# An MoE block on one core: four slots' expert rows go through DRAM and are fetched per token, in place of one-hot products

## The chip, the core and the metric

The kernel runs on one core of a Trainium2 chip. Times are device microseconds of one launch, from the first to the last instruction and what lies around them, as the runtime gives them. TensorE (PE) has two clock levels, 1.2 and 2.4 GHz; the profile gives the granted share of the higher one.

## What is computed

512 tokens of width 1024 pass a layer norm, a token mixer (convolution and pooling), a second layer norm that gives `h`, a mixture of 32 experts, a gated per-layer embedding and a last layer norm. The change is in the mixture:

```python
g_idx = top1(tok @ w_rg + b_rg)                      # one of 4 groups
top_v, top_i = top_k(e_logits_of_that_group, 2)      # two of its 8 experts
act = silu(tok @ w_gate[e]) * (tok @ w_up[e]) * combine[e]
moe = sum_e act @ w_down[e]                          # two experts per token
ple = (p @ w_ple) * sigmoid(h @ w_pg + b_pg)
out = layernorm(alpha * h + moe + ple)
```

An expert has 3 MB of float32 weights, all 32 have 96 MB, and each is read once.

## The kernel before, in words

Experts are ranked by how many tokens they have, and ranks are packed into 12 slots of 128 rows (`SLOTS`, from `ORDER_S`). A slot holds four experts of 32 rows ("q", and slot 0), two of 64 ("p"), or one of 96 and one of 32 ("h"). The slots run in the order 0, q, h, p, q, h, p, q, p, p, p, p, so slots 2 to 5 are h, p, q, h.

For each slot `s` the main loop does the following on PE. `gate_up` (L1043) multiplies the slot's gathered and transposed rows with the gate and up weights, in two halves of the contraction. `xtr` (L1032) transposes the next slot's rows. `act` makes the activation on ACT and DVE and, on DVE, a one-hot matrix `oh` of the tokens that the rows belong to (L1061). `atr` (L1066) transposes the activation. `down` (L1083) multiplies with the down weights; its result is copied out of PSUM by ACT as a rounded high part and by DVE as the low rest (L1091, L1093). One slot later `scatter` (L1105, L1107) takes the rows back to the 512 tokens: for each of 4 chunks of tokens and 2 halves of the width one product of `oh` with the high and one with the low part, 16 matmuls of 128x512 per slot, and DVE adds each PSUM result to `tok` (L1108). Chunks 0 and 1 stand between the halves of the next slot's `gate_up`, chunks 2 and 3 around its `atr`.

Weights come in pieces of 1 MB by SP's DMA queue (`pump`, L667; `W`, tile `w_x`), three for each expert, in the order of the slots. They are put into one of about 14 buffers, each given back (`done`) when PE has read it; `keep` holds some buffers back for other uses. A load waits for its buffer, and for the load eight issues earlier. Rows of the slot three ahead are gathered from DRAM (`h1d`) by an indirect DMA on POOL (`gather`, L1023), which skips rows that have no token.

The embedding gate's products (`q_pg`, L807, L815, L818) are filler: 160 "quanta", one product of 128x256 each, put between the other work. `fill(n)` places `n` of them. `fill_until(keys)` places as many as fit before a weight piece is expected, by the account `clk`: `clk["pe"]` adds up the assumed time of PE's work, `clk["dma"]` that of the loads. So the account, at build time, sets where the quanta stand; on the chip nothing is moved. 30 of them stand ahead of slot 0. At slot 9 `fill(999)` places all that are left, since later work needs the finished `tok`. From slot 9 on `tok` is also split into high and low parts for the last norm (`split_tok`), and slot 11 overlaps its own last steps with the norm and the stores.

## Time and profile before

| | us |
|---|---|
| median of 3 runs (lowest, highest) | 479.41 (478.61, 481.82) |
| the profiled execution | 477.51 |
| its span, first to last instruction | 475.7 |
| PE busy in the span | 444.1 |

The profile is of one execution. Engines are PE (matmul), PEld (its weight loads), DVE, ACT, POOL and SP; a "q" behind the name is the engine's sequencer, which issues DMAs. A matmul's modelled duration overlaps the next one's, so PE's work is best read from the starts in the timeline. The slots' part begins at 197 us and ends at about 463 us.

### The profile page before, as it was taken

The numbers are of one execution on the slowest core, as the hardware profiler recorded it, in microseconds if no ns is written. First come the engines' busy times: TensorE is split into PE (matmuls) and PEld (weight loads), VectorE is DVE, ScalarE is ACT, GpSimd is POOL, SyncE is SP. The second block draws the span as 40 slices with busy tenths as digits, with TensorE's granted clock in tenths as the row PEclk, the third lists the DMA queues.
The fourth block names the chain that finished last, engine by engine and source line by source line (L and its number), as shares of the span: only waits on it lengthen the run. The fifth ranks groups of instructions, "written<-read, shape, count | busy, mean of one in ns | idle before, by whom it ended". The sixth has DMA issues, their size and how long they took to land.

```text
span 475.7 us, 7009 instructions
## 1 busy us (share of the span) xinstructions
PE 444.1 (93%) x2647; PEld 297.7 (63%) x2647; DVE 253.4 (53%) x493; ACT 131.0 (28%) x240; POOL 141.8 (30%) x121
## 2 busy tenths in 40 slices
PE   7899979999999998898879999999999999999990
PEld 6798857788899997542425446644556458454430
DVE  4939599879664776322424422443433361354695
ACT  4562512341400585220202211211201121241260
POOL 2557499327403640320001000100001011432094
PEclk8999997999999998999989999999999999999995
DMA  8822204222876797499999999999999999486013
GB/s 265 340 91 89 90 1 167 99 100 96 332 285 253 250 352 282 161 372 421 416 425 419 420 418 421 420 421 418 418 422 420 421 417 417 182 252 234 1 44 148
DMA packets 23389, 133.20 MB, mean 280 GB/s; under 512 B 3329, under 2 KB 3589, under 8 KB 10040
## 3 DMA queue, kind: packets, MB, share of 16 engines
q1 hardware_dynamic: 20456, 124.64, 65.9%
q0 software_dynamic: 2608, 6.50, 3.6%
q10 hardware_dynamic: 288, 1.57, 0.8%
q8 instruction: 22, 0.36, 0.3%
q14 instruction: 15, 0.12, 0.1%
HBM read 130.41 MB, written 4.72 MB: 284 GB/s over the span
## 4 chain that ended last, share of the span: by engine, by line
PE 39%; DMA 14%; DVE 2%; issue 1%; ACT 1%; POOL 1%; POOLq 0%; SPq 0%; DVEq 0%; ACTq 0%
DMA w_x<-wx_in 14%; PE g_gu L1043 14%; PE q_pg L815 7%; PE u_y L1083 6%; PE u_sc L1105 4%; PE u_sc L1107 3%; PE q_pg L807 2%; PE t_xt L1032 2%; PE q_zr L1322 1%; PE t_at L1066 0%; DVE tok L1364 0%; POOL tok L1352 0%; DVE tok L1359 0%; ACT L1340 0%; POOLq L1545 0%
## 5 line engine op out<-in xcount | busy, mean ns | idle before, releaser
L1043 PE MATMUL g_gu<-w_x,xT 128*32 128x512 f32 (+1 forms) x544 | 84.0, 607 | 5.6 <-DMA w_x<-wx_in 5.4
L1108 DVE TENSOR_TENSOR tok<-tok,u_sc 128x512 f32<-128x512 f32 x88 | 55.3, 680 | 54.1 <-PE u_sc L1107 54.0
L360 PE MATMUL u_u<-hTh,ws 128*128 128x512 f32 (+1 forms) x320 | 67.6, 355 | 0.5 <-DVE ws L245 0.3
L360 PEld LDWEIGHTS u_u<-hTh,ws 128*128 128x128 f32 x320 | 53.9, 193 | 9.3 <-DVE ws L245 0.8
L1043 PEld LDWEIGHTS g_gu<-w_x,xT 128*32 128x32 f32 (+1 forms) x544 | 22.5, 119 | 56.8 <-issue 47.9
L815 PE MATMUL q_pg<-w_pg,h1T 128*128 128x256 f32 x240 | 58.1, 385 | 0.0
L815 PEld LDWEIGHTS q_pg<-w_pg,h1T 128*128 128x128 f32 x240 | 45.8, 193 | 9.1 <-issue 2.5
L1023 POOL DMA_INDIRECT xrow<-h1d,idxm x12 | 12.3, 1022 | 117.6 <-PE t_xt L1032 108.5
L1083 PE MATMUL u_y<-w_x,aT 128*32 128x512 f32 (+1 forms) x272 | 41.1, 596 | 0.0
L1105 PE MATMUL u_sc<-y,oh 128*128 128x512 f32 x88 | 40.4, 459 | 0.0
L826 POOL TENSOR_TENSOR tok<-tok,sgp 128x256 f32<-128x256 f32 x16 | 11.5, 724 | 85.4 <-DVE sgp L825 78.4
L184 PE MATMUL u_o<-ws,yTh 128*128 128x256 f32 x128 | 36.7, 287 | 0.3 <-ACT yTh L443 0.3
L186 PE MATMUL u_o<-ws,yTl 128*128 128x256 f32 x128 | 36.3, 284 | 0.6 <-DVE yTl L444 0.6
L360 PE MATMUL u_u<-hTl,ws 128*128 128x512 f32 (+1 forms) x160 | 35.3, 351 | 1.2 <-DVE hTl L345 1.2
L185 PE MATMUL u_o<-ws,yTh 128*128 128x256 f32 x128 | 36.2, 283 | 0.0
L1093 DVE TENSOR_TENSOR y<-u_y,y 128x512 fp32r<-128x512 f32 x22 | 15.2, 692 | 37.0 <-ACT y L1091 37.0
L1107 PE MATMUL u_sc<-y,oh 128*128 128x512 f32 x88 | 34.7, 394 | 0.0
L360 PEld LDWEIGHTS u_u<-hTl,ws 128*128 128x128 f32 x160 | 27.5, 192 | 5.7 <-DVE hTl L345 1.6
L1052 ACT ACTIVATE sa<-g_gu 128x256 f32<-128x256 f32 x12 | 4.6, 382 | 96.0 <-PE g_gu L1043 96.0
L245 DVE TENSOR_TENSOR ws<-raw,ws 128x1024 fp32r<-128x1024 f32 (+1 forms) x19 | 25.3, 1365 | 9.8 <-ACT ws L242 9.8
L1105 PEld LDWEIGHTS u_sc<-y,oh 128*128 128x128 f32 x88 | 16.6, 189 | 15.7 <-issue 8.2
L1055 DVE TENSOR_TENSOR sa<-g_gu,sa 128x256 f32<-128x256 f32 x12 | 5.1, 422 | 39.3 <-ACT sa L1052 39.3
(273 smaller groups left out, 682.9 us busy)
## 6 DMA issues: line engine op xcount, KB each, us to landing
w_x<-wx_in SPq DMA_DIRECT2D x89, 1024.0 KB, 20.4
raw<-win_in SPq DMA_DIRECT2D x6, 1024.0 KB, 6.2
w_half<-wx_in SPq DMA_DIRECT2D x12, 512.0 KB, 7.3
raw<-wout_in SPq DMA_DIRECT2D x4, 1024.0 KB, 4.7
w_pg<-wpg_in SPq DMA_DIRECT2D x4, 1024.0 KB, 20.2
raw<-win_in SPq DMA_DIRECT2D x4, 512.0 KB, 6.8
bc<-rows_in SPq DMA_DIRECT2D x4, 512.0 KB, 9.6
h1d<-tok POOLq DMA_DIRECT2D x3, 512.0 KB, 7.2
```

Source lines behind the costliest of these rows:

```text
L184: PE.matmul(o, lh, rh, start=start, stop=False)
L185: PE.matmul(o, lh, rl, start=False, stop=False)
L186: PE.matmul(o, ll, rh, start=False, stop=stop)
L245: eng.tensor_sub(wsp[n][1][j][:, ks], raws[n][:, j, ks], wsp[n][0][j][:, ks].bitcast(F32))
L360: PE.matmul(o[:, ns], (l if p == 2 else h)[j][:, kn], (hTl if p == 1 else hTh)[k][:, ns], start=i == 1, stop=i == 3 * KD)
L815: PE.matmul(g, h1T[:, k, cs], W["pg", j, 0][0][:, k * 256:(k + 1) * 256], start=(k == 0), stop=False)
L1043: PE.matmul(g[q:q + m, :], xTs[s][:, k, q:q + m], W["x", r, kh][0][:, (k % 4) * 512:(k % 4 + 1) * 512], start=(k == 0), stop=(k == KD - 1) ...
L1083: PE.matmul(yp[h][q:q + m, :], aTs[s][:, c, q:q + m], W["x", r, 2][0][:, c * D + h * 512:c * D + (h + 1) * 512], start=(c == 0), stop=(c = ...
L1093: V.tensor_sub(yl[:, hs], yp[h], yh[:, hs].bitcast(F32))
L1105: PE.matmul(o, ohs[s][:, c * P:(c + 1) * P], yh[:, w], start=True, stop=yl is None)
L1107: PE.matmul(o, ohs[s][:, c * P:(c + 1) * P], yl[:, w], start=False, stop=True)
L1108: V.tensor_add(tok[:, c, w], tok[:, c, w], o)
```

## The change

Slots 2 to 5 (`DS`) are no longer scattered by one-hot products. `down` copies their rows (ACT the first half, DVE the second) into one half of the tile `yrows`, and ACT's queue writes them to the DRAM tensor `yd`, 512 KB for each slot. Slot indices of each token's two experts are put into `yix`, shifted so that those outside slots 2 to 5 lie out of bounds. For each chunk of 128 tokens, `blank` zeroes a tile of two rows per token on ACT (in a weight buffer), `fetch` reads the rows of `yd` by two indirect DMAs on POOL, which skip indices out of bounds, and `collect` adds the two to `tok` on DVE (128x1024 each). Chunks 0 and 1 are blanked and fetched in slot 6 and added in slot 7; chunks 2 and 3 are blanked and fetched behind slot 7 and added in slot 8. `keep` holds back two buffers from slot 5 on for that. The other slots keep the one-hot products.

The account's numbers are changed (3.7 in place of 3.45, and so on; the start of the slots' account is -1.5 ahead of slot 0 where it was 8.0 behind it), so that quanta are placed elsewhere.

```diff
@@ -70,6 +70,8 @@
 NS = len(SLOTS)
 NOV = 8
 NL = NS + 1
+DS0, DS1 = 2, 6
+DS = range(DS0, DS1)
 MORE = NS * P - 32
 
 
@@ -177,6 +179,7 @@
     eps_t = const.tile([P, 1], F32, name="eps_t")
     sgn = const.tile([P, 1], F32, name="sgn")
     h1d = dram.tile([1 + T, D], F32, name="h1d")
+    yd = dram.tile([len(DS) * P, D], F32, name="yd")
     SLOT = {}
 
 
@@ -968,12 +971,14 @@
     V.scalar_tensor_tensor(g5, g5, BIG, pos3[:, :, 0:NST], OP.mult, OP.add)
     V.scalar_tensor_tensor(g4, g5, float(MORE), g4, OP.add, OP.min)
     gq = sm("gq", 2 * NC, E)
+    glist = {}
 
     def lists(gp, iotas, ns, nm, oq):
 
         V.tensor_tensor(gq.rearrange("p (i c) e -> p i c e", i=2), A12,
                         gp.unsqueeze(1).broadcast_to([P, 2, NC, E]), OP.mult)
         gi, si = sm("gi", 2 * NC, 1, dt=I32), sm("si", 2 * NC, 1, dt=I32)
+        glist[nm] = gi
         with nc.allow_low_precision(reason="whole numbers"):
             V.tensor_reduce(gi, gq, AX.X, OP.add)
         V.tensor_scalar(si, gi, 7, None, OP.arith_shift_right)
@@ -1043,7 +1048,7 @@
                 PE.matmul(g[q:q + m, :], xTs[s][:, k, q:q + m],
                           W["x", r, kh][0][:, (k % 4) * 512:(k % 4 + 1) * 512],
                           start=(k == 0), stop=(k == KD - 1), tile_position=(0, q))
-        clk["pe"] += 3.45
+        clk["pe"] += 3.7
         done(*[("x", r, kh) for r in dict.fromkeys(r for _, _, r in lanes)])
 
     def act(s, wsl, tkf, i, oh=None, sa=None):
@@ -1057,6 +1062,8 @@
         acts[s] = sa
         if s == NS - 1:
             return
+        if s in DS:
+            return
         ohs[s] = tmp("cv", 2, [P, T], f"oh{s}", F32R) if oh is None else oh
         V.tensor_scalar(ohs[s], C["iota"], tkf[:, i:i + 1], None, OP.is_equal)
 
@@ -1071,7 +1078,11 @@
         if s == NS - 1:
             y2 = ys[s] = tmp("x2", 1, [P, 2, 512], f"y{s}")
         else:
-            if y2 is None:
+            if s in DS:
+                if s == DS0:
+                    ys["d"] = tmp(ytags[0], 1, [P, 2, D], "yrows")
+                y2 = ys["d"][:, s % 2, :]
+            elif y2 is None:
                 y2 = tmp(ytags[0], 1, [P, 2, D], f"y{s}", F32R)
                 ys[s] = yh, yl = y2[:, 0, :], y2[:, 1, :]
             else:
@@ -1088,11 +1099,37 @@
             if s == NS - 1:
                 A.copy(y2[:, h, :], yp[h])
                 continue
+            if s in DS:
+                (A.copy if h == 0 else V.tensor_copy)(y2[:, hs], yp[h])
+                continue
             A.copy(yh[:, hs], yp[h])
             if yl is not None:
                 V.tensor_sub(yl[:, hs], yp[h], yh[:, hs].bitcast(F32))
-        clk["pe"] += 3.6
+        if s in DS:
+            A.dma_start(yd[(s - DS0) * P:(s - DS0 + 1) * P, :], y2)
+            clk["dma"] += 1.25
+        clk["pe"] += 3.75
         done(*[("x", r, 2) for r in dict.fromkeys(r for _, _, r in lanes)])
+
+    ygs = {}
+
+    def blank(c):
+
+        tag = free.pop(0) if c < 2 else ygs[c - 2][1]
+        yg = tmp(tag, 1, [P, 2, D], f"yg{c}")
+        ygs[c] = (yg, tag)
+        A.mul(yg.rearrange("p i (a n) -> p (i a) n", a=2), C["iota"].unsqueeze(1).broadcast_to([P, 4, 512]), 0.0)
+
+    def fetch(c):
+        clk["dma"] += 0.9
+        for i in range(2):
+            G.indirect_dma_start(out=ygs[c][0][:, i, :], out_offset=None, in_=yd,
+                                 in_offset=bass.IndirectOffsetOnAxis(ap=yix[:, i * NC + c, :], axis=0),
+                                 bounds_check=len(DS) * P - 1, oob_is_err=False)
+
+    def collect(c):
+        for i in range(2):
+            V.tensor_add(tok[:, c, :], tok[:, c, :], ygs[c][0][:, i, :])
 
     def scatter(s, cs=range(NC), mid=None, hs=(0, 1)):
         yh, yl = ys[s]
@@ -1106,7 +1143,7 @@
                 if yl is not None:
                     PE.matmul(o, ohs[s][:, c * P:(c + 1) * P], yl[:, w], start=False, stop=True)
                 V.tensor_add(tok[:, c, w], tok[:, c, w], o)
-            clk["pe"] += 0.88
+            clk["pe"] += 1.15
 
     xrow = [tmp(f"x{i}", 1, [P, D], f"xrow{i}") for i in range(2)]
     eid = s32("eid", 1, dt=I32)
@@ -1170,6 +1207,10 @@
     for gated, _ in hold[1:]:
         gated()
     wsl = slot_weights(oq, osl, NL, "m", tmp("cv", 2, [P, T], "oqb").bitcast(BF16))
+
+    yix, yin = sm("yix", 2 * NC, 1, dt=I32, tag="L"), sm("yin", 2 * NC, 1, tag="mg")
+    V.tensor_scalar(yin, glist["m"], float(DS0 * P), BIG, OP.is_lt, OP.mult)
+    V.scalar_tensor_tensor(yix, glist["m"], -float(DS0 * P), yin, OP.add, OP.add)
 
     def reload(spare):
         for k in spare:
@@ -1445,16 +1486,20 @@
     gather(2, idx, 2)
     pump()
     fill(FILLB)
+    clk["pe"] = -1.5
     gate_up(0, SLOTS[0], 0)
     fill(FILLC)
     gate_up(0, SLOTS[0], 1)
-    clk["pe"] = 8.0
     for s in range(NS):
         lanes = SLOTS[s]
         rs = list(dict.fromkeys(r for _, _, r in lanes))
         end = s == NS - 1
         if s in KEEP:
             keep[0] = KEEP[s]
+        if s == DS1:
+            keep[0] = 0
+            for c in range(2):
+                blank(c)
         if s == NS - 3:
             fill(999)
             last_load()
@@ -1477,7 +1522,8 @@
             gate_up(s, lanes, 0)
             if s == NS - 4:
                 t = token_row(t)
-            scatter(s - 1, (0, 1))
+            if s - 1 not in DS:
+                scatter(s - 1, (0, 1))
             if s == NS - 4:
                 selectors(t)
                 keep[0] = 2
@@ -1495,14 +1541,28 @@
         xtr(s + 1)
         if s + 3 < NS:
             gather(s + 3, idx, s + 3)
-        if s:
+        if s == DS1:
+            for c in range(2):
+                fetch(c)
+        if not s:
+            fill(FILL0)
+        elif s - 1 in DS:
+            fill(FILLD)
+        else:
             scatter(s - 1, (2,))
-        else:
-            fill(FILL0)
         atr(s)
-        clk["pe"] += 1.2
-        if s:
+        clk["pe"] += 1.35
+        if s and s - 1 in DS:
+            fill(FILLD)
+        elif s:
             scatter(s - 1, (3,), lambda: fill(MIDF))
+        if s == DS1 + 1:
+            for c in range(2):
+                collect(c)
+        if s == DS1 + 2:
+            for c in range(2, 4):
+                collect(c)
+                free.append(ygs[c][1])
         if s == NS - 3:
             split_tok(2, G)
             split_tok(3, G)
@@ -1511,9 +1571,14 @@
         if s == NS - 2:
             take(s - 1, ys[s - 1])
         down(s, lanes)
-
-
-KEEP = {NS - 4: 3}
+        if s == DS1 + 1:
+            for c in range(2, 4):
+                blank(c)
+                fetch(c)
+
+
+KEEP = {DS1 - 1: 2, NS - 4: 1}
+FILLD = 2
 MIDF = 4
 LNP = 512
 WLAG = 2.0
```

The three pieces below show how this comes out. On PE in slot 3 (`t_at` is the transposed activation, `u_sc` a scatter product, `q_pg` filler, `u_y` the down product), the rows from `atr` to the first down product were, before:

```order
L1066 MATMUL t_at_3068<-par,sa_3038 128x128 x2
L1105 MATMUL u_sc_3073<-y_2970,oh_2920 128x512
L1107 MATMUL u_sc_3073<-y_2970,oh_2920 128x512
L815 MATMUL q_pg_2967<-w_pg_0_1755,h1T 128x256 x4
L1105 MATMUL u_sc_3081<-y_2970,oh_2920 128x512
L1107 MATMUL u_sc_3081<-y_2970,oh_2920 128x512
L815 MATMUL q_pg_2967<-w_pg_0_1755,h1T 128x256 x2
L1083 MATMUL u_y_3088<-w_x_2_2817,aT_3071 64x512
```

On the same engine and place they are now:

```order
L1037 MATMUL t_xt_3053<-par,xrow_1888 128x128 x4
L818 MATMUL q_pg_2981<-w_pg_0_1756,h1T 128x256 x2
L1073 MATMUL t_at_3064<-par,sa_3042 128x128 x2
L818 MATMUL q_pg_2981<-w_pg_0_1756,h1T 128x256 x4
L821 MATMUL q_pg_2981<-bpg,bm 128x256
L1094 MATMUL u_y_3077<-w_x_2_2825,aT_3067 64x512
```

The scatter products are gone, and filler alone covers the wait for the activation. On PE between slot 8's down product and slot 9's first `gate_up` (`g_gu`) there stood, before, among others:

```order
L1083 MATMUL u_y_3966<-w_x_2_3712,aT_3944 64x512
L807 MATMUL q_pg_3982<-wple_3190,pT_1077 128x256
L807 MATMUL q_pg_3982<-wple_3190,pT_1078 128x256
L815 MATMUL q_pg_3982<-w_pg_0_2821,h1T 128x256 x8
L818 MATMUL q_pg_3982<-bpg,bm 128x256
L807 MATMUL q_pg_3997<-wple_3190,pT_1077 128x256
L807 MATMUL q_pg_3997<-wple_3190,pT_1078 128x256
L815 MATMUL q_pg_3997<-w_pg_0_2821,h1T 128x256 x8
L818 MATMUL q_pg_3997<-bpg,bm 128x256
```

Now, on PE at that place, the two follow each other:

```order
L1144 MATMUL u_sc_3902<-y_3738,oh_3673 128x512
L1094 MATMUL u_y_3911<-w_x_2_3643,aT_3896 64x512
L1094 MATMUL u_y_3911<-w_x_2_3645,aT_3896 64x512
L1094 MATMUL u_y_3911<-w_x_2_3643,aT_3896 64x512
L1094 MATMUL u_y_3911<-w_x_2_3645,aT_3896 64x512
L1094 MATMUL u_y_3912<-w_x_2_3643,aT_3896 64x512
L1094 MATMUL u_y_3912<-w_x_2_3645,aT_3896 64x512
L1094 MATMUL u_y_3912<-w_x_2_3643,aT_3896 64x512
L1094 MATMUL u_y_3912<-w_x_2_3645,aT_3896 64x512
L1048 MATMUL g_gu_3940<-w_x_0_3647,xT_3869 64x512
```

All 30 quanta that stood there have moved ahead of slot 8. On DVE in slot 8 (`tok<-tok,u_sc` adds a scatter product, `y` is the low part of the slot's own down product) there was, before:

```order
L1056 SCALAR_TENSOR_TENSOR sa_3911<-g_gu_3853,sa_3911 128x256
L1061 TENSOR_SCALAR oh_3915<-par,tkfm 128x512
L1108 TENSOR_TENSOR tok<-tok,u_sc_3933 128x512
L1108 TENSOR_TENSOR tok<-tok,u_sc_3937 128x512
L1108 TENSOR_TENSOR tok<-tok,u_sc_3946 128x512
L1108 TENSOR_TENSOR tok<-tok,u_sc_3954 128x512
L825 TENSOR_TENSOR sgp_3797<-q_pg_3796,sgp_3797 128x256
L1093 TENSOR_TENSOR y_3964<-u_y_3965,y_3964 128x512
L1093 TENSOR_TENSOR y_3964<-u_y_3966,y_3964 128x512
```

On DVE in slot 8 there is now, with the additions of fetched rows (`yg`):

```order
L1061 SCALAR_TENSOR_TENSOR sa_3863<-g_gu_3796,sa_3863 128x256
L1068 TENSOR_SCALAR oh_3867<-par,tkfm 128x512
L1145 TENSOR_TENSOR tok<-tok,u_sc_3885 128x512
L1145 TENSOR_TENSOR tok<-tok,u_sc_3889 128x512
L1145 TENSOR_TENSOR tok<-tok,u_sc_3898 128x512
L1145 TENSOR_TENSOR tok<-tok,u_sc_3902 128x512
L1132 TENSOR_TENSOR tok<-tok,yg_3778 128x1024 x2
L1132 TENSOR_TENSOR tok<-tok,yg_3786 128x1024 x2
L1107 TENSOR_TENSOR y_3910<-u_y_3911,y_3910 128x512
L1107 TENSOR_TENSOR y_3910<-u_y_3912,y_3910 128x512
```

The four additions of fetched rows stand ahead of the low part that slot 8's scatter needs in slot 9.

## Rows read from the trace of the kernel before

**Rows 1.** The page: busy time of the engines; granted clock and DMA in slices.

```profile
PE 444.1 (93%) x2647; PEld 297.7 (63%) x2647; DVE 253.4 (53%) x493; ACT 131.0 (28%) x240; POOL 141.8 (30%) x121
...
PEclk8999997999999998999989999999999999999995
DMA  8822204222876797499999999999999999486013
```

**Rows 2.** Busy time by stretch: us, the engines, granted clock, DMA share, GB/s.

```profile
247.00:374.00 127.00, 127.00 (x767) 68.87 (x765) 48.87 (x86) 21.07 (x44) 11.85 (x14) 1.00 1.01 420
374.00:407.00 33.00, 32.68 (x153) 21.15 (x151) 12.84 (x34) 4.04 (x9) 3.18 (x4) 1.00 0.99 412
407.00:445.00 38.00, 37.98 (x172) 17.63 (x172) 17.17 (x27) 10.06 (x17) 12.60 (x12) 1.00 0.54 185
...
239.00:247.00 8.00, 6.53 (x35) 1.80 (x36) 0.00 (x0) 0.00 (x0) 0.00 (x0) 0.79 1.02 424
```

**Rows 3.** Waits of SP's queue: us in total, times, longest.

```profile
SPq L667 <- DMA w_x<-wx_in: 105.6, 59, 2.7
```

**Rows 4.** Timeline of PE at slots 1 and 2: start, us, idle before.

```profile
222.65 3.62 PE L1043 MATMUL g_gu<-w_x,xT 128*32 128x512 f32 x26 [1.44 <-DMA w_x<-wx_in]
...
239.05 1.06 PE L1043 MATMUL g_gu<-w_x,xT 128*32 128x512 f32 x6 [2.50 <-DMA w_x<-wx_in]
241.53 4.92 PE L1043 MATMUL g_gu<-w_x,xT 128*32 128x512 f32 x26 [1.42 <-DMA w_x<-wx_in]
...
248.55 3.64 PE L1043 MATMUL g_gu<-w_x,xT 128*32 128x512 f32 x32
```

**Rows 5.** Timeline of PE in slot 6: eight scatter products, then gate_up.

```profile
330.84 0.50 PE L1105 MATMUL u_sc<-y,oh 128*128 128x512 f32 x1
...
333.01 3.65 PE L1043 MATMUL g_gu<-w_x,xT 128*64 128x512 f32 x16
```

**Rows 6.** Timeline of PE: first of slot 9's 30 quanta, then its gate_up.

```profile
393.57 1.13 PE L807 MATMUL q_pg<-wple,pT 128*128 128x256 f32 x4
...
407.07 3.65 PE L1043 MATMUL g_gu<-w_x,xT 128*64 128x512 f32 x16
```

**Rows 7.** Timeline of SP's queue: single issues of weight pieces.

```profile
281.40 0.33 SPq L667 DMA_DIRECT2D w_x<-wx_in  x1
...
372.97 0.33 SPq L667 DMA_DIRECT2D w_x<-wx_in  x1
...
375.46 0.33 SPq L667 DMA_DIRECT2D w_x<-wx_in  x1
...
385.40 0.33 SPq L667 DMA_DIRECT2D w_x<-wx_in  x1
```

**Rows 8.** Timeline of PE: slot 4's first gate_up; slot 8's second, and its `atr`.

```profile
282.24 3.64 PE L1043 MATMUL g_gu<-w_x,xT 128*32 128x512 f32 x32
...
380.09 3.65 PE L1043 MATMUL g_gu<-w_x,xT 128*64 128x512 f32 x16
...
386.01 0.41 PE L1066 MATMUL t_at<-par,sa 128*128 128x128 f32 x2 [0.32 <-DVE sa L1056]
```

**Rows 9.** DMA issues: count, KB each, median us from issue to landing.

```profile
w_x<-wx_in SPq DMA_DIRECT2D x89, 1024.0 KB, 20.4
...
h1d<-tok POOLq DMA_DIRECT2D x3, 512.0 KB, 7.2
...
xrow<-h1d,idxm POOLq DMA_INDIRECT x12, 9.1
```

**Rows 10.** Groups by line and shape: count, busy us, mean ns, idle before.

```profile
L1120 ACT ACTIVATE xrow<-tok 128x1024 f32<-128x1024 f32 x2 | 2.0, 1046 | 0.0
...
L751 DVE TENSOR_TENSOR tok<-tok,bc 128x1024 f32<-128x1024 f32 x1 | 1.2, 1216 | 0.0
...
L1023 POOL DMA_INDIRECT xrow<-h1d,idxm x12 | 12.3, 1022 | 117.6 <-PE t_xt L1032 108.5 <-DVE gsum L1147 8.6 <-issue 0.3
```

**Rows 11.** Timeline of DVE in slot 8: its first scatter additions; the low part.

```profile
386.20 1.86 DVE L1108 TENSOR_TENSOR tok<-tok,u_sc 128x512 f32<-128x512 f32 x3
...
392.64 0.69 DVE L1093 TENSOR_TENSOR y<-u_y,y 128x512 fp32r<-128x512 f32 x1 [1.71 <-ACT y L1091]
```

## The prediction

> **What bounds the kernel now.** I read the page first: PE is busy for 93% of the span, but DMA stands at 9 tenths or more through half of the slices [rows 1]. So the next view is busy time by stretch. From 247 to 374 us PE has no idle time at all, and the DMA engines are full too, at 420 GB/s. From 374 to 407 both are still full. From 407 to 445 PE is full and DMA falls to half [rows 2]. The waits of SP's queue say what a load waits for: mostly an earlier load (105.6 us in 59 waits), not a buffer [rows 3]. So until about 407 us weights arrive at a fixed rate. PE keeps pace because filler is placed into its waits, and afterwards PE alone sets the end.
>
> The slack of the loads shows who leads. A load is issued when the one eight issues earlier has landed, so an issue's time is a landing time. Slot 8's second gate_up starts at 380.09 [rows 8]; its two pieces landed at 372.97 and 375.46 [rows 7], 4.63 us before. Slot 9's pieces are in at 385.40 [rows 7], but its gate_up starts at 407.07, because 13.50 us of filler stand ahead of it [rows 6]: 21.7 us of slack. The end therefore moves if filler leaves that place, and the loads let it move by about 20 us at most.
>
> **The change part by part.** All times are for the profiled execution (477.51).
>
> Scatter. Eight products take 333.01 - 330.84 = 2.17 us with their spacing [rows 5], so 16 take 4.34 and four slots' 64 take 17.4. This is PE time on the path. Their 32 additions on DVE go too (three take 1.86 us [rows 11], 32 take 19.8), but DVE had room: 48.87 us busy of 127 [rows 2].
>
> Filler. 30 quanta take 13.50 us, 0.45 each [rows 6]. Counted in the two orders, slots 0 to 9 had 10, 6, 6, 6, 24, 9, 6, 24, 9, 30 and now have 10, 9, 15, 6, 36, 13, 11, 30, 0, 0. So 39 (17.6 us) move ahead of slot 8, and from slot 8's second gate_up on 36 are gone, 16.2 us.
>
> DMA. Four writes of 512 KB are 2.10 MB, 5.0 us at 420 GB/s. The fetches skip absent tokens; by the reference's routing on its inputs slots 2 to 5 hold 59, 80, 92 and 55 rows, 286 of 4 KB, 1.17 MB, 2.8 us, of which 148 rows (1.45 us) go in slot 6. By slot 8's second gate_up the loads are thus later by E = 5.0 + 1.45 = 6.45 us. The trace has no write under full load. From below it costs 0, if it passes beside the reads. From above it costs the whole 7.2 us that a write of `h1d` from POOL took to land [rows 9], 28.8 for four. I take the bytes, since loads come 375.46 - 372.97 = 2.49 us apart for 1.05 MB [rows 7] while each needs 20.4 to land [rows 9]: times to land overlap, bytes do not. A fetch DMA is bounded by 0 and by all its 128 rows (1.25 us); I take the rows present, which lie between.
>
> The page DMA: Bandwidth & Descriptors of the Trainium skill (section Anatomy of one DMA) gives a transfer a fixed 2 us beside its bytes. Charged to the engines, a write would be 3.2 us by an estimate from that page, E would be 14.3, and the sum 7.8 us worse. The trace speaks against charging it so, with loads 2.49 us apart.
>
> ACT, DVE and POOL. A blank is two rows of 1046 ns [rows 10]; four make 8.4 us on an ACT that is 28% busy [rows 1]. A fetch DMA is 1.0 us of POOL [rows 10], eight are 8.2. POOL waits for slot 5's write ahead of the first fetch, and behind it stand filler additions that nobody needs soon. An addition of fetched rows is taken as 1.22 us [rows 10], eight are 9.7, half of what DVE loses. The copies of rows cost what the casts and low parts did.
>
> Only in slot 8 has DVE no room. Count from its second gate_up: before, the scatter additions began 386.20 - 380.09 = 6.1 later, and now they do too. Four of them (2.5), four of fetched rows (4.9) and two low parts (0.69 each [rows 11]) end at +14.9, the first low part at +14.2. PE does `atr` at +5.9 [rows 8], then four products, the down product and slot 9's first gate_up (1.1 + 3.6 + 3.6), so it asks for the low parts from +14.4 on. I take 0.5 for that. The fetches must have landed by +8.6; they are issued behind blanks of 2.1 us, from about 2 ahead of this gate_up to 1 behind it, and take 9.1 [rows 9], so the last is in at about +10, when the additions reach it. Two small index operations ahead of slot 0 are put at 0.3. The two buffers held back cost nothing as long as eight loads stay outstanding.
>
> The walk, as delay of PE against before:
> - Slot 2: PE idled 2.50 and 1.42 there, and the 26 matmuls behind took 4.92 [rows 4], where 26/32 of 3.64 is 2.96. Twelve more quanta (5.4) fill the idle time. The load still lands at 241.53, but the low clock goes: -2.0.
> - Slot 3: a scatter goes, filler is equal: -6.3.
> - Slot 4: six more quanta ahead of its first gate_up bring PE there at 282.24 [rows 8] - 3.6 = 278.6. The last of its four pieces landed at 281.40 [rows 7]; one or two writes make it 282.7 to 283.9. PE waits 4 to 5 us, and the loads lead: +1.6 by the second half.
> - From there to slot 8's second gate_up two and a half scatters (10.9) go and 18 quanta (8.1) come: PE alone would be at -1.2.
> - The loads say 375.46 + 6.45 = 381.9 there, +1.8. Waits on slot 7's pieces leave PE a little behind that: +2.5.
> - From there 16.2 less: -13.7. With 0.5 and 0.3: -12.9.
> - Slot 9's pieces land at 385.40 + 7.8 = 393.2 and are asked for at 394.2, so they just do not hold it up. Later ones have more room.
>
> Forecast: 477.5 - 12.9 = 464.6. The median of the runs was 1.9 above the profiled execution, so I predict 466.5.
>
> **The rivals** (times on the scale of the median).
> 1. More gain. If the writes pass beside the reads, E is 1.45: slot 8's second gate_up can start at 376.9, -3.2, and the sum is -18.6: 460.8. For it: the full engines all read. Against it: the same engines get more bytes.
> 2. The clock. PE will wait ahead of some six half-slots in slots 4 to 8. If each wait is followed by a low clock worth 1.96 us, as at 241.53, that is 11.8, of which some 3.5 is time in which PE would wait for loads anyway: -12.9 + 8.3 = -4.6, 474.8. For it: from 239 to 247 the granted clock was 0.79 [rows 2]. Against it: after a wait of 1.44 at 222.65 the 26 matmuls took 3.62 [rows 4]. The page TensorE: Matmul & The Clock Gate of the Trainium skill (Part 1) says that sustained activity gives the full clock and idleness takes it back; the trace agrees in one of the two places.
> 3. Late fetches. If those of chunks 2 and 3, issued at about 383, land after 20.4 as loads do, and not after 9.1 [rows 9], DVE stands in slot 8 for 11 us more, and slot 9's first scatter waits for its low part: -2, 477.4. Against it: all twelve gathers had a median of 9.1, most of them beside full loads.
> 4. Slower. The four writes in slots 2 to 5 hold up the loads for all of their time to land, 7.2 us each: E = 30.3, slot 8's second gate_up starts at 405.8, 23.2 later than in the walk, and the sum is +10.3: 489.7. It decides once E passes 6.45 + 12.9 = 19.4, which is 4.5 us per write. Against it: landing overlaps, as above.
>
> **How the numbers follow.** The forecast has 0.69, rival 1 0.12, rival 2 0.07, rival 3 0.06, rival 4 0.06. One per cent (4.8 us) is about what a measurement tells from no change. Faster by more: 0.69 + 0.12 + half of rival 2 (0.04) = 0.85. Within it: the other half and rival 3, 0.09. Slower: 0.06. The range runs from near rival 1 (461.0) to a forecast in which the first four fetches cost all their rows (5.0 in place of 1.45, +3.5) and one or two waits lower the clock (+3): 473.0.
>
> **What would show it.** Right: `u_sc` has 112 products in place of 176; no filler behind 380; slot 9's gate_up starts near 394; PE idles ahead of slot 4's; DMA stays at 420 GB/s from 217 to about 415; the fetches land within 10 us. Wrong: gate_up in slots 4 to 8 waits for loads by much more than 5 us, DVE idles ahead of the additions of `yg` in slot 8, or the clock falls below 0.95 between 280 and 390.

## The result, and the profile after

| us | before | after |
|---|---|---|
| median (lowest, highest; runs) | 479.22 (478.61, 481.82; 4) | 465.96 (465.60, 468.95; 4) |
| the profiled execution | 477.51 | 465.60 |
| its span | 475.7 | 463.6 |

The ratio is 0.9727, with a 95% interval of 0.9673 to 0.9781: faster. Measured again beside other kernels, the changed one had a median of 467.35 against 478.75, ratio 0.9772 (0.9735 to 0.9810).

The page of the changed kernel, beside [rows 1]: busy time of the engines, the group of scatter products, clock and DMA in slices.

```profile
PE 428.5 (92%) x2583; PEld 287.6 (62%) x2583; DVE 239.2 (52%) x463; ACT 136.0 (29%) x240; POOL 149.7 (32%) x129
...
PEclk9999998999999999999999998999999999999995
DMA  8822203422769669669999999999999999999213
...
L1142 PE MATMUL u_sc<-y,oh 128*128 128x512 f32 x56 | 25.5, 456 | 0.0
```

PE is busy for 15.6 us less. There are 56 products on each of the two scatter lines, 112 in all, where 176 stood. DMA is full (9) until three slices later than before.

Busy time by stretch, the stretches of [rows 2], in the changed kernel (columns as there):

```profile
247.00:374.00 127.00, 123.12 (x723) 66.85 (x719) 26.12 (x46) 22.32 (x43) 17.29 (x20) 0.99 1.02 419
374.00:407.00 33.00, 31.23 (x151) 14.23 (x143) 24.81 (x48) 11.69 (x16) 10.14 (x11) 1.00 1.02 416
407.00:445.00 38.00, 37.98 (x167) 17.75 (x166) 20.87 (x42) 12.84 (x22) 12.42 (x10) 1.00 0.66 264
239.00:247.00 8.00, 8.00 (x58) 3.40 (x60) 2.48 (x4) 0.00 (x0) 0.00 (x0) 1.00 1.01 420
```

The idle time and the low clock at slot 2 are gone (last row: 8.00 busy at full clock, 6.53 at 0.79 before). New idle time stands between 247 and 374 (3.9 us) and between 374 and 407 (1.8 us). The timeline of PE shows where, in slots 1, 2, 4, 7, 8 and 9:

```profile
212.57 3.62 PE L1048 MATMUL g_gu<-w_x,xT 128*32 128x512 f32 x32
...
239.15 4.29 PE L1048 MATMUL g_gu<-w_x,xT 128*32 128x512 f32 x32
...
277.75 1.05 PE L1048 MATMUL g_gu<-w_x,xT 128*32 128x512 f32 x4
279.21 1.05 PE L1048 MATMUL g_gu<-w_x,xT 128*32 128x512 f32 x2 [0.41 <-DMA w_x<-wx_in]
282.44 5.32 PE L1048 MATMUL g_gu<-w_x,xT 128*32 128x512 f32 x26 [2.18 <-DMA w_x<-wx_in]
292.32 3.68 PE L1048 MATMUL g_gu<-w_x,xT 128*32 128x512 f32 x32
...
347.68 1.06 PE L1048 MATMUL g_gu<-w_x,xT 128*32 128x512 f32 x6
349.40 3.62 PE L1048 MATMUL g_gu<-w_x,xT 128*32 128x512 f32 x26 [0.67 <-DMA w_x<-wx_in]
...
359.01 1.06 PE L1048 MATMUL g_gu<-w_x,xT 128*32 128x512 f32 x6
360.70 3.62 PE L1048 MATMUL g_gu<-w_x,xT 128*32 128x512 f32 x26 [0.62 <-DMA w_x<-wx_in]
...
382.07 3.65 PE L1048 MATMUL g_gu<-w_x,xT 128*64 128x512 f32 x16
...
393.04 3.80 PE L1048 MATMUL g_gu<-w_x,xT 128*64 128x512 f32 x16
398.70 0.50 PE L1144 MATMUL u_sc<-y,oh 128*128 128x512 f32 x1 [1.43 <-DVE y L1107]
400.67 3.65 PE L1048 MATMUL g_gu<-w_x,xT 128*64 128x512 f32 x16
```

Slot 4 waits for weights, and its next 26 matmuls take 5.32 where 3.62 is usual. Slot 7 waits twice. The idle time in brackets is only a part of such a loss: slot 7's two halves take 5.34 and 5.31 from their first to their last product (347.68 to 353.02, 359.01 to 364.32), where 32 products in one piece take 3.64. Slot 4's 26 products took longer than those of slot 7 because of the clock, as the stretches show (columns as above), first slot 4's, then those at 349.40:

```profile
282.40:287.80 5.40, 5.36 (x27) 1.34 (x28) 0.00 (x0) 0.00 (x0) 0.00 (x0) 0.68 1.03 428
349.40:353.00 3.60, 3.60 (x27) 0.95 (x27) 0.00 (x0) 0.00 (x0) 0.02 (x1) 1.00 1.01 407
```

Slot 9's gate_up starts at 393.04, where it was 407.07 [rows 6]. In the middle of slot 9 PE waits for a low part from DVE. The timeline of DVE at that place, which answers to [rows 11]:

```profile
388.17 2.46 DVE L1145 TENSOR_TENSOR tok<-tok,u_sc 128x512 f32<-128x512 f32 x4
390.55 2.48 DVE L1132 TENSOR_TENSOR tok<-tok,yg 128x1024 f32<-128x1024 f32 x2
393.74 1.22 DVE L1132 TENSOR_TENSOR tok<-tok,yg 128x1024 f32<-128x1024 f32 x1 [0.71 <-DMA yg<-yd,yix]
396.82 1.23 DVE L1132 TENSOR_TENSOR tok<-tok,yg 128x1024 f32<-128x1024 f32 x1 [1.85 <-DMA yg<-yd,yix]
397.96 1.28 DVE L1107 TENSOR_TENSOR y<-u_y,y 128x512 fp32r<-128x512 f32 x2
```

The additions of fetched rows take 1.22 each, as taken, but they wait 2.56 us for two fetches, and the low parts stand behind them. The DMA issues (us from issue to landing, beside [rows 9]) and the waits of SP's queue (beside [rows 3]) say what the rows' DMAs met:

```profile
w_x<-wx_in SPq DMA_DIRECT2D x89, 1024.0 KB, 17.3
...
xrow<-h1d,idxm POOLq DMA_INDIRECT x12, 8.9
...
yg<-yd,yix POOLq DMA_INDIRECT x8, 13.0
```

```profile
SPq L670 <- DMA w_x<-wx_in: 96.9, 49, 5.1
SPq L670 <- DMA yd<-yrows: 25.5, 3, 9.6
```

The last fetch is issued at 382.70. The load issued at 381.29 shows that the last piece for slot 8's second gate_up has then landed, as 375.46 does in [rows 7]:

```profile
382.70 1.00 POOL L1126 DMA_INDIRECT yg<-yd,yix  x1 [0.30 <-issue]
```

```profile
381.29 2.83 SPq L670 DMA_DIRECT2D w_x<-wx_in  x2
```

A fetch of `yg` lands after 13.0 us (median) and not after 9.1. And SP's queue stood 25.5 us behind writes of `yd`, up to 9.6 at once, while DMA kept 419 GB/s in the stretch from 247 to 374.

One difference has nothing to do with slots 2 to 5. Busy time from 178 to 190 us, ahead of the slots, first before, then after:

```profile
178.00:190.00 12.00, 10.75 (x66) 8.63 (x65) 7.84 (x35) 6.45 (x9) 0.50 (x3) 0.86 0.75 291
```

```profile
178.00:190.00 12.00, 10.75 (x75) 8.66 (x75) 9.31 (x46) 6.86 (x11) 1.53 (x4) 1.00 0.75 297
```

PE is busy for the same 10.75 us in both, the clock is 0.86 and 1.00, and the slots' part starts 1.40 us earlier after (196.10, not 197.50). The control below has 0.86 there too. Times of one kernel differ by up to some 5 us. In the profiles a part of that lies ahead of slot 1, whose first gate_up starts between 211.95 and 216.01 at nearly equal code, so the experiments are also compared from slot 1's first gate_up on.

### The profile page after: what moved, and what is told of

Its sections match the earlier page's. It is cut to its first block, busy times and chain, and to the rows that moved or that the text cites. A ratio compares the mean times of both kernels' runs of the same rounds, so it can differ in the third digit from the quotient of the medians.

```text
span 463.6 us, 6886 instructions
## 1 busy us (share of the span) xinstructions
PE 428.5 (92%) x2583; PEld 287.6 (62%) x2583; DVE 239.2 (52%) x463; ACT 136.0 (29%) x240; POOL 149.7 (32%) x129
## 4 chain that ended last, share of the span: by engine, by line
PE 24%; DMA 23%; issue 5%; DVE 1%; POOL 1%; SPq 1%; ACT 1%; POOLq 0%; DVEq 0%; ACTq 0%
DMA w_x<-wx_in 20%; PE g_gu L1048 10%; PE q_pg L818 4%; PE u_y L1094 3%; DMA yg<-yd,yix 3%; PE u_sc L1142 2%; PE t_xt L1037 1%; PE u_sc L1144 1%; PE q_zr L1363 1%; PE q_pg L810 1%; SPq L670 0%; SPq L664 0%; DVE tok L1405 0%; PE t_at L1073 0%; POOL yg L1126 0%
## 5 line engine op out<-in xcount | busy, mean ns | idle before, releaser
L1048 PE MATMUL g_gu<-w_x,xT 128*32 128x512 f32 (+1 forms) x544 | 88.1, 610 | 5.5 <-DMA w_x<-wx_in 5.2
L1048 PEld LDWEIGHTS g_gu<-w_x,xT 128*32 128x32 f32 (+1 forms) x544 | 25.5, 119 | 58.1 <-issue 44.9
L1145 DVE TENSOR_TENSOR tok<-tok,u_sc 128x512 f32<-128x512 f32 x56 | 35.1, 680 | 29.1 <-PE u_sc L1144 28.9
L818 PEld LDWEIGHTS q_pg<-w_pg,h1T 128*128 128x128 f32 x240 | 44.5, 190 | 8.1 <-issue 2.5
L828 DVE TENSOR_TENSOR sgp<-q_pg,sgp 128x256 f32<-128x256 f32 x15 | 6.3, 423 | 42.0 <-ACT sgp L825 41.9
L245 ACT CAST ws<-raw 128x1024 fp32r<-128x1024 f32 x23 | 23.1, 1046 | 8.6 <-DMA raw<-wout_in 5.4
L1142 PE MATMUL u_sc<-y,oh 128*128 128x512 f32 x56 | 25.5, 456 | 0.0
L1094 PEld LDWEIGHTS u_y<-w_x,aT 128*32 128x32 f32 (+1 forms) x272 | 11.7, 117 | 22.1 <-issue 21.0
## 6 DMA issues: line engine op xcount, KB each, us to landing
w_x<-wx_in SPq DMA_DIRECT2D x89, 1024.0 KB, 17.3
```

Source lines behind the costliest of these rows:

```text
L245: copy(wsp[n][0][j], raws[n][:, j, :])
L818: PE.matmul(g, h1T[:, k, cs], W["pg", j, 0][0][:, k * 256:(k + 1) * 256], start=(k == 0), stop=False)
L1048: PE.matmul(g[q:q + m, :], xTs[s][:, k, q:q + m], W["x", r, kh][0][:, (k % 4) * 512:(k % 4 + 1) * 512], start=(k == 0), stop=(k == KD - 1) ...
L1094: PE.matmul(yp[h][q:q + m, :], aTs[s][:, c, q:q + m], W["x", r, 2][0][:, c * D + h * 512:c * D + (h + 1) * 512], start=(c == 0), stop=(c = ...
L1142: PE.matmul(o, ohs[s][:, c * P:(c + 1) * P], yh[:, w], start=True, stop=yl is None)
L1145: V.tensor_add(tok[:, c, w], tok[:, c, w], o)
```

## The experiments

Starts in us counted from slot 1's first gate_up, each in its profiled execution: slot 8's second gate_up (8b), slot 9's second (9b), and the end of the span.

| kernel | 8b | 9b | end |
|---|---|---|---|
| before | 166.1 | 198.8 | 261.7 |
| after | 169.5 | 188.1 | 251.0 |
| after again | 169.1 | 187.2 | 250.3 |
| 30 quanta held back | 169.7 | 200.0 | 263.6 |
| no rows | 163.7 | 180.4 | 243.0 |
| no fetches | 167.0 | 183.7 | 246.5 |
| rows written twice | 174.5 | 193.0 | 256.0 |
| late additions | 170.1 | 188.7 | 253.2 |
| early fetch | 170.6 | 188.3 | 251.3 |
| slots 2 to 4 only | 170.8 | 188.2 | 251.2 |
| after, old account | 172.7 | 190.3 | 253.3 |
| before, new account | 161.8 | 195.9 | 258.7 |
| early fetch, split | 170.0 | 187.7 | 254.5 |
| all rows fetched | 172.4 | 194.1 | 257.0 |

**Filler held back.** Is it the products' removal or the filler that moves into it?

```diff
-        if not quanta:
+        if len(quanta) <= HOLDQ:
             return False
...
+HOLDQ = 30
```

> The kernel after, but the last 30 quanta of filler are held back to slot 9, where the kernel before had 30. Theory A (the loads set the time up to slot 8's second gate_up, so what the scatter's removal frees is worth something only through the filler that moves into it): the 13.5 us of filler return ahead of slot 9, slot 8's second gate_up can start only about 0.8 earlier than after (its pieces land at 381.3, it starts at 382.07), and the 1.9 us that slot 9 lost to late fetches go: +10.8, 476.8. Rival B (64 products less are 17.4 us less, wherever the filler stands): no change, 466.

Measured: 479.29, ratio 1.0017 (0.9978 to 1.0056). Its PE timeline in slot 7, where the filler is missing:

```profile
349.43 1.16 PE L1048 MATMUL g_gu<-w_x,xT 128*32 128x512 f32 x2 [2.13 <-DMA w_x<-wx_in]
352.44 5.90 PE L1048 MATMUL g_gu<-w_x,xT 128*32 128x512 f32 x26 [1.85 <-DMA w_x<-wx_in]
...
363.72 3.62 PE L1048 MATMUL g_gu<-w_x,xT 128*32 128x512 f32 x26 [1.76 <-DMA w_x<-wx_in]
```

The whole gain is gone: 8b stands where it stood (169.7), and the time that the filler leaves goes into waits for loads. Theory A holds and rival B does not; A's 476.8 was 2.5 low.

**No rows, no fetches, rows written twice.** What do the rows' DMAs cost the loads? The run without rows leaves out both issues below, the run without fetches only the second.

```diff
-            A.dma_start(yd[(s - DS0) * P:(s - DS0 + 1) * P, :], y2)
...
-            G.indirect_dma_start(out=ygs[c][0][:, i, :], out_offset=None, in_=yd,
...
```

> The rows are neither written nor fetched (both DMA issues left out; the blanked tiles are still added), so slots 2 to 5 are missing from the output; all else as after. Theory A (row transfers take the loads' bytes, E = 6.45 us up to slot 8's second gate_up): PE's waits and low clock of slots 4 to 7 go, 0.41 + 2.18 + 0.67 + 0.62 + 2.36 = 6.2, and the 1.9 us of slot 9: -8.1, 457.9. Rival 1 of the prediction (writes pass beside the reads): only the fetches' share goes, 1.45 and 1.9: 462.6. Rival C (PE leads in slots 4 to 8, loads do not matter): 464.1.

> The rows are written but not fetched (the blanked tiles are still added), so slots 2 to 5 are missing from the output. Theory A (a fetch costs the rows that it brings, 148 rows or 1.45 us ahead of slot 8, and the late ones 1.9 us in slot 9): -3.3, 462.6. Rival D (a fetch costs all of its 128 rows, 1.25 us each, also the skipped ones): -5.0 - 1.9 = -6.9, 459.1. If only lateness costs: 464.1.

```diff
+    yd2 = dram.tile([len(DS) * P, D], F32, name="yd2")
...
             A.dma_start(yd[(s - DS0) * P:(s - DS0 + 1) * P, :], y2)
+            A.dma_start(yd2[(s - DS0) * P:(s - DS0 + 1) * P, :], y2)
```

> Each slot's rows are written twice, the second time to a DRAM tensor that nobody reads: four more writes of 512 KB. Theory A (bytes, 1.25 us each): slot 7 waits 5.0 longer, +5.0, 471.0. Rival 1 (writes beside reads): 466. Rival E (2 us fixed beside the bytes, 3.2 each): +12.8, 478.8. Rival 4 (7.2 us each): +28.8, 494.8.

Measured: 458.46, 463.79 and 473.01. In the table the end moves by -8.0, -4.5 and +5.0, where theory A had -8.1, -3.3 and +5.0. The medians are 0.5 to 2.3 us above that, and in these profiles slot 1 starts 1.8 to 3.4 later than in the profile after, at equal code ahead of it; by the median alone the run without fetches would lie nearest to 464.1, lateness alone. PE's waits for weights from 270 to 400 us, in the three (first without rows, then without fetches, then with rows written twice):

```profile
PE g_gu L1048 <- DMA w_x<-wx_in: 2.0, 2, 1.2
```

```profile
PE g_gu L1048 <- DMA w_x<-wx_in: 2.3, 1, 2.3
```

```profile
PE g_gu L1049 <- DMA w_x<-wx_in: 7.2, 4, 2.6
```

Four more writes move 8b by 174.5 - 169.5 = 5.0: 1.25 each, their bytes. So a write neither passes beside the reads nor holds them up for its landing (three writes whose landing this trace shows took 7.7 to 8.3 us), though SP's queue waits for it: the DMA engines stayed full meanwhile, at 417 GB/s from 247 to 400. The Trainium skill (DMA: Bandwidth & Descriptors, section Anatomy of one DMA) gives some 2 us fixed beside the bytes, for transfers on GpSimd's path, and puts most of them down to the wait for completion. The trace agrees that full engines are not charged with them: by an estimate that charges them to each write, the run would have been 478.8. Without fetches 8b is 2.5 earlier (2.1 against the control), and slot 9 saves another 1.9 (9b - 8b: 16.7, not 18.6). That 8b moves as well leaves lateness alone out. Without rows 8b is 5.8 earlier; PE then waits in slot 4 alone, so that is about the most the loads could give.

**All rows fetched.** What is skipping worth?

```diff
     V.tensor_scalar(yin, glist["m"], float(DS0 * P), BIG, OP.is_lt, OP.mult)
-    V.scalar_tensor_tensor(yix, glist["m"], -float(DS0 * P), yin, OP.add, OP.add)
+    V.tensor_scalar(yix, glist["m"], len(DS) * P - 1, None, OP.bitwise_and)
```

> The indices of absent tokens are folded into the tensor's 512 rows in place of out of bounds, so each fetch brings all of its 128 rows (the output then holds rows of other tokens). 364 rows more in slot 6 (1.49 MB) and 374 more in slots 7 and 8. Theory A (a fetch costs the bytes of the rows that it brings, at 420 GB/s): +3.5 up to slot 8's second gate_up, and the late fetches land up to 3.6 later, as long as DVE waits for them in slot 8: +7.1, 473.1. Rival D (skipped rows cost as much as rows brought): 466.

Measured: 474.43. DVE in slot 8 of this kernel:

```profile
398.34 1.23 DVE L1132 TENSOR_TENSOR tok<-tok,yg 128x1024 f32<-128x1024 f32 x1 [3.09 <-DMA yg<-yd,yix]
402.18 1.22 DVE L1132 TENSOR_TENSOR tok<-tok,yg 128x1024 f32<-128x1024 f32 x1 [2.61 <-DMA yg<-yd,yix]
```

8b moves by 2.9 (3.3 against the control; 3.5 expected) and 9b by 6.0 (7.1 expected), and DVE's waits grow from 2.56 to 5.70. Bringing the 364 skipped rows of slot 6 costs nearly their bytes, so skipping them costs little; rival D is out.

**Late additions, early fetch, both halves.** Can slot 9's 1.9 us be had? In the first, chunks 2 and 3 are added behind the low parts. In the second they are fetched ahead of slot 7's down product. In the third, besides, chunk 3 is added in slot 9.

```diff
-        if s == DS1 + 2:
-            for c in range(2, 4):
-                collect(c)
-                free.append(ygs[c][1])
...
         down(s, lanes)
+        if s == DS1 + 2:
+            for c in range(2, 4):
+                collect(c)
+                free.append(ygs[c][1])
```

> The additions of chunks 2 and 3 stand behind slot 8's low parts on DVE, not ahead of them. Theory A (in slot 9 PE waited for low parts that stood behind additions that waited 0.71 and 1.85 for their fetches): slot 9's products find their low parts in time; the four additions then reach from about 394 to 398 and slot 8's scatter additions begin behind them, 1.2 earlier than the 399.24 of after: -1.2, 464.8. Rival F (the wait in slot 9 has another cause, or DVE stands as long at the new place): 466.

```diff
         if s == DS1 + 1:
             for c in range(2):
                 collect(c)
+                blank(c + 2)
+                fetch(c + 2)
...
         down(s, lanes)
-        if s == DS1 + 1:
-            for c in range(2, 4):
-                blank(c)
-                fetch(c)
```

> The blanks and fetches of chunks 2 and 3 are issued in slot 7 right behind the additions that free their buffers, ahead of slot 7's down product, not behind it. Theory A: the last fetch is issued near 378 and not at 382.7 and lands near 392, before DVE asks for it at 393; slot 9's 1.9 us go: -1.9, 464.1. Rival G (a fetch lands after the loads that were issued ahead of it, whenever it is issued, so an earlier issue holds up a load by as much; ACT's blanks ahead of slot 7's row copies hold up slot 8's products): 466 or more.

```diff
         if s == DS1 + 2:
-            for c in range(2, 4):
-                collect(c)
-                free.append(ygs[c][1])
+            collect(2)
+            free.append(ygs[2][1])
...
             if s - 1 not in DS:
                 scatter(s - 1, (0, 1))
+            if s == DS1 + 3:
+                collect(3)
+                free.append(ygs[3][1])
```

> The early fetch, and the two additions of chunk 3 moved from slot 8 to behind slot 9's first scatter additions on DVE. Theory A (with the fetches early it is DVE's own work ahead of slot 8's low parts that holds up slot 9): the low parts end 2.4 earlier, before PE asks for them, and from slot 8's second gate_up to slot 9's second it is 16.7 as in the run without fetches, where the early fetch alone had 17.7: -1.0 against the early fetch alone, 466.4. If PE was late there for another reason: 467.4.

Measured: 468.24 (ratio 0.9783, 0.9744 to 0.9822), 467.45 (0.9767, 0.9732 to 0.9802) and 471.11 (0.9839, 0.9804 to 0.9874), where the control has 0.9772. None gains: the first two come nearest to rivals F and G, and the third lies above both of its forecasts. Each shifts the wait. With late additions, PE's timeline in slot 9 and the stretch behind it:

```profile
402.12 0.50 PE L1142 MATMUL u_sc<-y,oh 128*128 128x512 f32 x1 [1.69 <-DVE tok L1145]
402.78 5.35 PE L1048 MATMUL g_gu<-w_x,xT 128*64 128x512 f32 x16
```

```profile
402.80:408.20 5.40, 5.40 (x18) 1.58 (x18) 3.40 (x3) 1.99 (x2) 2.36 (x1) 0.68 1.02 426
```

The wait for the low part has become one for a scatter addition, 1.69 long, and the granted clock behind it is 0.68. With the early fetch DVE no longer waits, but slot 9's first gate_up does. Tile `w_x` from 394 to 402 in that kernel, idle time by what ended it:

```profile
  DMA w_x<-wx_in: 0.9, 1
```

The fetch issued earlier takes a load's place, which is rival G. In the third kernel the additions moved to slot 9 run beside POOL's split of `tok`:

```profile
402.94 4.52 DVE L1132 TENSOR_TENSOR tok<-tok,yg 128x1024 f32<-128x1024 f32 x2
```

```profile
403.05 3.33 POOL L1319 TENSOR_TENSOR tokl<-tok,tokh 128x1024 fp32r<-128x1024 f32 x1 [10.83 <-ACT tokh L1318]
```

```profile
409.60 0.41 PE L1073 MATMUL t_at<-par,sa 128*128 128x128 f32 x2 [2.04 <-DVE sa L1061]
```

Two additions take 4.52 where they took 2.48, and PE waits for the activation behind them. The first takes the usual 1.22 (it ends at 404.16); the second takes the rest and ends 1.08 behind POOL's split:

```profile
404.19 3.27 DVE L1132 TENSOR_TENSOR tok<-tok,yg 128x1024 f32<-128x1024 f32 x1
```

**Slots 2 to 4 only.** One write and one slot's rows less, one scatter more.

```diff
-DS0, DS1 = 2, 6
+DS0, DS1 = 2, 5
```

> Slot 5 is scattered by products again; slots 2 to 4 go through DRAM, and blanks, fetches and additions each come one slot earlier. Theory A: one write (1.25) and 55 rows in part (0.3) fewer ahead of the loads, the 16 products (4.34) fall into PE's waits of slots 4 to 7 (6.2 with the low clock), two quanta (0.9) go behind slot 8's gate_up, and DVE's wait in slot 8 goes (1.9), since the last additions now stand in slot 7: -2.6, 463.4. Rival H (PE leads in slots 5 to 8 and the products cost their time): +4.3 + 0.9 - 1.9, 469.3.

Measured: 468.01, ratio 0.9780 (0.9748 to 0.9812), as the control. Neither theory holds. DVE's wait is gone (9b - 8b is 17.4, with two quanta more in it), but 8b is at 170.8. PE waits for loads in slot 4 (2.3 us of idle), and slot 7's second half shows that one of its pieces came late too, since it takes 4.79 and not 3.64:

```profile
361.51 4.79 PE L1048 MATMUL g_gu<-w_x,xT 128*32 128x512 f32 x32
```

Behind it PE leads: 8b starts 2.5 after its last piece has landed (by the load issued then), where that is 0.8 in the changed kernel. So with three slots or four in DRAM, PE and the loads are within some two microseconds of each other there.

**The account alone.** The account's old numbers on the changed kernel, and its new ones on the kernel before:

```diff
-        clk["pe"] += 3.7
+        clk["pe"] += 3.45
...
-    clk["pe"] = -1.5
...
+    clk["pe"] = 8.0
```

> The kernel after with the account's numbers of the kernel before (3.45, 3.6, 0.88, 1.2, and 8.0 behind slot 0). By the build's order 11 quanta then leave slot 2's wait and stand in slots 6 to 8. Theory A: those quanta (12 more behind slot 4, 5.4 us) lie on PE's path behind slot 4, less the waits of 1.3 in slot 7 that they fill: +4.1, 470.1. Rival I (the account's numbers are worth nothing beside the freed products): 466.

> The kernel before with the account's numbers of the changed one, its scatter untouched. By the build's order slot 2's wait takes 11 quanta more, and 39 instead of 36 stand behind slot 8's second gate_up. Theory A: the waits and the low clock of slot 2 go, but slot 8's second gate_up can come forward only by the slack of its pieces, 4.63 at most, and waits ahead of slot 4 with a low clock of about 2 take some back; three quanta more behind it cost 1.35: -3.2, 475.2. Rival J (the account is the whole gain, the products' removal adds nothing): 466. Rival K (the account is worth nothing without the freed products): 478.4.

Measured: 470.78 (ratio 0.9849, 0.9809 to 0.9890) and 474.85 (0.9919, 0.9894 to 0.9944). Both medians are near theory A, and rivals I, J and K are out; in the table, though, the old account costs 2.3 at the end where 4.1 was expected, and that includes a low clock at slot 2 which the expectation did not have. PE's timeline at slot 2 with the old account:

```profile
239.27 1.06 PE L1048 MATMUL g_gu<-w_x,xT 128*32 128x512 f32 x6 [2.70 <-DMA w_x<-wx_in]
241.75 6.59 PE L1048 MATMUL g_gu<-w_x,xT 128*32 128x512 f32 x26 [1.43 <-DMA w_x<-wx_in]
```

The wait and the low clock of [rows 4] are back. By the table's end the products' removal alone is worth 261.7 - 253.3 = 8.4, the account alone 3.0, both 10.7.

**A control.**

> The changed kernel unaltered, as a control on the chip of the next three. In its profile and in those of the other experiments the slots' part begins 0.4 to 2.4 us apart at equal code, with a low clock ahead of slot 0 or in it. From slot 1's first gate_up to the end of the span the changed kernel took 251.0 and the kernel before 261.7; that difference, 10.7, should hold here within 0.5, whatever the time of the run, which may be 1 to 2 us above 466.0 (466 to 468) if the low clock falls into it.

Measured: 467.35, and 250.3 from slot 1 on, 0.7 below the first profile and so just outside the 0.5. No variant that still does all of the work is measurably faster than the changed kernel.

## Why the prediction was right, and where its steps were off

The time came out at 465.96 for a predicted 466.5, and the mechanism is the one named: the gain is filler moved from behind slot 8 into time that the products left, bounded by the loads. Holding the filler back takes all of it away. The time of the profiled execution fell by 11.9 for a predicted 12.9, and 1.4 of the 11.9 is the clock ahead of the slots, which was not in the working. From slot 1 on it is 10.7 for 13.2. That the median came within 0.5 is in part luck: the slots gained 2.5 less than forecast, the clock ahead of them gave 1.4, and the median lay 0.4 above the profiled execution and not the 1.9 that were added.

| delay of PE against before, from slot 1 on | predicted | measured |
|---|---|---|
| slot 2's second gate_up | -2.0 | -1.5 |
| slot 4's first gate_up | -3.6 | -3.1 |
| slot 4's second | +1.6 | +1.3 |
| slot 8's second | +2.5 | +3.4 |
| slot 9's first | -13.7 | -12.6 |
| slot 9's second | -13.2 | -10.7 |

- Slot 2: the mechanism is right. The load still sets the place, the low clock is gone. Its price was too high: the prediction put it at 4.92 less 26/32 of 3.64, which is 1.96. But 26 products behind a wait take 3.62 at a granted clock of 1.00 (at 349.40 and 360.70), as 32 do without one (3.64): by the order of the products, all those of the expert that comes last are then still to be done. So the low clock was worth 4.92 - 3.62 = 1.30, and rival 2's 1.96 for each wait was too high as well.
- Slot 4: PE reached it nearly as predicted (-3.1 for -3.6). Its first half took 10.01 us (277.75 to 287.76) where 3.64 is usual. Of these 6.37, 1.70 are a low clock (5.32 - 3.62, granted clock 0.68), and the other 4.67 are the late pieces, within the 4 to 5 that were predicted; 2.59 of them show as idle time. The low clock is rival 2, in one of the three halves in which PE waited. It does not seem to reach slot 8's second gate_up, since PE runs into the loads again: in the profile of the late additions slot 4's 26 products took 3.62, and 8b was no earlier (170.1). The Trainium skill (TensorE: Matmul & The Clock Gate, Part 1) has idleness take the clock back; the trace agrees in slot 4, but behind slot 7's waits of 0.67 and 0.62 the 26 products took the usual 3.62.
- E, writes: 1.25 each, as taken; rivals 1 and 4 are out.
- E, fetches: the term that was too small. The rows of slot 6's fetches were put at 1.45; leaving them out moves 8b by 2.1 to 2.5. With the writes' 5.0 that makes E 7.1 to 7.5, and the landing of slot 8's last piece did move by 7.2, not 6.45 (381.29 is 168.7 from slot 1 on, where 375.46 was 161.5). All rows in their place cost 2.9 to 3.3 for 364 rows, near their bytes (3.5). What the rest of 0.7 to 1.1 is stays open.
- Slot 8 on DVE: the step that failed. The late fetches, says the prediction, "take 9.1 [rows 9], so the last is in at about +10, when the additions reach it". The last was issued at 382.70, 0.6 behind slot 8's second gate_up and so where it was expected, but it landed 14.0 later. The median over the kernel is 13.0. The last addition began 14.8 behind slot 8's second gate_up (396.82 - 382.07), and from there to slot 9's second it is 14.1 less than before (32.7 to 18.6) for a predicted 15.7. That is rival 3 at a small size: not 11 us of standing but 2.56. The 9.1 came from gathers issued singly over the whole kernel. Each later one of a group lands later: the four fetches of slot 6, issued 1.3 apart beside full loads, landed 10.8, 13.0, 15.3 and 17.3 after their issues, the last three of slot 7 10.8, 12.3 and 14.0.
- Index operations: 0.3 taken. Slot 0 began at 197.87 in the run without rows and at 197.50 before, both with the low clock at 178 to 190: about 0.4.
- From slot 9's second gate_up to the end it is 62.9 in both, as taken.
- The signs: the 112 products, the place of slot 9's gate_up (393.04), no filler behind 380 and DMA at 419 GB/s from 217 to 415 came as written. The fetches did not land within 10 us, and one sign of being wrong came: DVE idles ahead of the additions of `yg` in slot 8. It cost 1.9 us and not the gain.

## What to carry to other kernels

Work taken off a full engine is worth only what can be put in its place: find what else stands behind the point where the loads cease to lead, and move that. In this kernel, with the DMA engines full, an added write on another queue cost its bytes and a fetch somewhat more than those of its rows; a fetch's landing is to be priced by transfers issued in a like group at the same place, not by a median over the kernel. Idle time in front of a group of products can be less than half of what a late piece costs. Once loads, PE and DVE are within a microsecond or two of each other, shifting one step only names the next wait: four attempts on slot 9's 1.9 us gained nothing.

## What the runs showed that was not expected

- A load queue that stands 25.5 us behind writes cost nothing beyond the writes' 5.0 us of bytes, since DMA stayed at 419 GB/s.
- Two DVE additions of 128x1024 took 4.52 us beside a POOL operation of 3.33 on the same tensor, and 2.48 in slot 8 of the changed kernel. The Trainium skill (SBUF — State Buffer, section Who interferes with whom) says that DVE and GpSimd share a port pair that one of them holds for a whole instruction. The trace agrees: POOL's split took 3.33 beside the first addition and 2.37 in the changed kernel, and the second addition, which takes 1.22 alone, ended 1.08 behind POOL's split. DVE's loss of 2.05 is thus about what was left of POOL's operation (2.19). The changed kernel has the same in slot 9, where DVE's own split takes 2.36 and again ends 1.08 behind POOL's; in the third variant it takes 1.21.

```profile
401.74 2.37 POOL L1319 TENSOR_TENSOR tokl<-tok,tokh 128x1024 fp32r<-128x1024 f32 x1 [11.68 <-ACT tokh L1318]
402.83 2.36 DVE L1319 TENSOR_TENSOR tokl<-tok,tokh 128x1024 fp32r<-128x1024 f32 x1 [1.11 <-ACT tokh L1318]
```

- Nearly equal code had a granted clock of 0.86 or 1.00 from 178 to 190 us in different executions. Before and after, that goes with 1.4 us at the start of the slots, the size of what the late additions (1.2) and the early fetch (1.9) were expected to gain.
